# One start address for all streamed operands, and one for all kept ones, in the MLP and the output projection

## The chip, the cores and the metric

The kernel runs on one core of one Trainium2 chip. The metric is the device time of one execution in microseconds (us), as the median of several runs. A profile is one execution of its own; its span runs from the core's first instruction to its last. A core has TensorE (PE; its weight loads are listed apart as PEld), VectorE (DVE), ScalarE (ACT), GpSimd (POOL) and SyncE (SP), which issues the transfers. The engines run their own instructions in order and wait for each other by semaphores. On-chip memory has 128 partitions; an address here is a byte offset within a partition, the same in all 128. "Residue" means the address mod 256.

## The reference, cut to what matters

One decoder layer in float32 over 272 tokens (16 meta tokens and 256 real ones) of width 2048:

```
u    = rmsnorm(h) ;  proj = u @ w_in                # 2048 x 6144
o    = differential attention (8 heads) and stick-breaking attention (8 heads)
mixed = concat(rmsnorm(o_diff) * 0.8, rmsnorm(o_sb))
h    = h + mixed @ w_out                            # 2048 x 2048
m    = rmsnorm(h)
hid  = square(relu(m @ w_up))                       # 2048 x 8192
h    = h + hid @ w_down                             # 8192 x 2048
```

The output is h for the 256 real tokens.

## The kernel before

**Products in three parts.** Every large operand x is split into hi (x rounded to the matrix unit's float32r) and lo = x - hi. A product of two operands is three matmuls into the same accumulator, a *trio*: hi by hi, and hi by lo in both ways. A matmul has a *kept* operand (`lhsT`, 128 columns, loaded by a weight load ahead of it) and a *streamed* one (`rhs`, 256, 272 or 512 columns of 4 bytes).

**Weights in pieces.** All weights come in pieces of 128 x 1024 floats (512 KB). SyncE loads a piece into one of five `raw` buffers (L232); ScalarE rounds it into `whi` (L179), VectorE subtracts it into `wlo` (L181). The split pieces stand in rings of three buffers, in the MLP of five. A ring buffer has 1024 + 4 x 16 floats, so that a piece may begin 0, 64 or 128 bytes into it: `offset(g)` gives this for each piece.

**Stages.** (1) The input projection "in" streams `u` and keeps the weights (L983 to L985), with the attention heads worked in between. (2) The output projection "out", about 340 to 433 us: it keeps 128 tokens of `mixed` and streams 512 columns of `w_out` (`triple`, L1074). (3) The MLP in 8 rounds of 1024 hidden features. "up" keeps weights and streams 256 tokens of `m` (`triple2`, L1068). "down" keeps 128 tokens of the hidden activations and streams weights (`triple`, L1074), in 22 of 32 units by a fast scheme of 7 products of 256 columns in place of 8 (pieces "a" and "b", for which VectorE also makes sums of weights and activations), in the other units by plain products of 512 columns. Up pieces of round r+1 and down pieces of round r alternate in an order written out by hand (`order`, `mix`); which job each engine is given when comes from `Pace`, a small planner with a cost per operation. Neither looks at addresses.

**Writers of the kept operands.** In "out", a head's norm writes `mixed[:, k]`, 256 elements for hi and 256 for lo. In the MLP, `up_evac` writes the hidden activations of one group of features in eight slots of 128 tokens: ScalarE copies 8 x 128 elements into hi (L897), VectorE subtracts into lo (L899). Before, all hi parts of `mixed` and of `hid` stand first and all lo parts after them, 16 floats further than they would need to (`two_parts`). `m` has the layout of `u`: hi at 0 and lo 272 floats further.

**Accumulator copies.** In the fast down scheme ScalarE copies accumulators out and in again between units (L930, L935).

Of the kernel before, what the change touches and what calls it, by code (L numbers as in the profile page):

```python
# [7 lines left out]
F32 = mybir.dt.float32  # L8
F32R = mybir.dt.float32r
# [4 lines left out]
P = 128  # L14
DM = 2048
SEQ = 256
META = 16
TOK = META + SEQ
KT = DM // P
EPS = 1e-6  # L20
NEG = -1e30
ROW = 576
LINE = 16
ROUNDS = 8
PAIRS = 4
# [97 lines left out]
def hymba_layer(ctx: ExitStack, tc: tile.TileContext, xT_d, xh_d, win_d, wout_d, wup_d, wdn_d, cst_d, par_d, out_d):  # L123
    nc = tc.nc
    cp = ctx.enter_context(tc.tile_pool(name="const", bufs=1))
    big = ctx.enter_context(tc.tile_pool(name="big", bufs=1))
    wp = ctx.enter_context(tc.tile_pool(name="weights", bufs=1))
# [25 lines left out]
    def retile(tag, shape, name):  # L153
        return rtile(tag, shape, name, SLOTS["e"])

    def two_parts(x, k, n):

        return x[:, :, : k * n].rearrange("p a (k n) -> p k a n", n=n)


    par = cp.tile([P, G_END], F32, name="par")
    cst = tp.tile([P, C_ID], F32, bufs=1, name="cst")
# [1 line left out]
    xT = big.tile([P, KT, TOK], F32, tag="x", name="xT")  # L164
    big.tile([P, LINE], F32, name="pad_act")
    um = big.tile([P, KT, ROW], F32R, tag="act", name="u")[:, :, : 2 * TOK].rearrange("p k (a n) -> p k a n", a=2)
    big.tile([P, 2 * LINE], F32, name="pad_mix")
    mixed = two_parts(big.tile([P, 2, KT * SEQ + LINE], F32R, tag="mix", name="mixed"), KT, SEQ)

    def split_u(k):  # L170
        g = par[:, G_MIX + k : G_MIX + k + 1]
# [13 lines left out]
    strips = []  # L185
# [35 lines left out]
    def source(g):  # L221
        what, *at = order[g]
        if what == "in":
            (_, a, b), c = strips[at[0]], at[1]
            return win_d[a, b][:, 4 * c : 4 * c + 4]
        return {"out": wout_d, "up": wup_d, "a": wdn_d}[what][tuple(at)]

    raws, parts, raw_at, done_at, parted = {}, {}, {}, {}, set()
    dma = [1700.0]

    def load(dst, src, n):
        nc.sync.dma_start(dst, src)  # L232
        dma[0] = max(dma[0], pc.pe + 1700) + n * 1.42
        return dma[0] + 400

    def fetch(number, pieces=1):
        if number < len(loads):
            g = loads[number]
            if not raws:
                wp.tile([P, 3 * LINE], F32, name="pad_w")  # L240
            raws[g] = wp.tile([P, 4, 256], F32, tag="raw", bufs=RAW, name=f"raw_{g}")
            n = 4 // pieces
            for i in range(pieces):
                k = slice(n * i, n * i + n)
                raw_at[g, i] = load(raws[g][:, k], source(g)[:, k], n * 256)
                yield

    ring = {g: g - PARTS for g in range(len(order))}

    def offset(g):  # L250

        what, *at = order[g]
        if what == "in":
            return LINE if strips[at[0]][1] in (0, 3) else 0
        return LINE if what == "up" and at[1:] in ([0, 0], [2, 0]) else 0  # L260

    def part(g, pieces=1):
        if g < len(order) and g not in parts:
            pool, bufs, tag = wp, PARTS, "w"
            if g >= first_mlp:
                ring[g] = max(g - MLP_PARTS, first_mlp - PARTS + (g - first_mlp) % MLP_PARTS) if (g - first_mlp) % MLP_PARTS < PARTS else g - MLP_PARTS
                if (g - first_mlp) % MLP_PARTS >= PARTS:
                    pool, bufs, tag = mp, MLP_PARTS - PARTS, "v"
                    ring[g] = ring[g] if g - MLP_PARTS >= first_mlp else -1
            at = offset(g)  # L270
            hi, lo = (
                pool.tile([P, 1024 + 4 * LINE], F32R, tag=tag + x, bufs=bufs, name=f"w{x}_{g}")[:, n : n + 1024]
                .rearrange("p (k n) -> p k n", k=4)
                for x, n in (("hi", at), ("lo", at + LINE))
            )
            parts[g] = (hi, lo)
            what, *at = order[g]
            fast = what in "ab" and (at[0], at[1]) in FAST
            pc.job("weights", (fast_a if what == "a" else fast_b)(g, hi, lo) if fast else halves(g, hi, lo, pieces))
# [31 lines left out]
    def halves(g, hi, lo, pieces):  # L311
        n = 4 // pieces
        for i in range(pieces):
            src = (g, i) if (g, i) in raw_at else (g, 0)
            while src not in raw_at or ring[g] >= 0 and ring[g] not in done_at:
                yield pc.pe + 200, None
            yield max(raw_at[src], done_at.get(ring[g], 0.0)), "a"
            k = slice(n * i, n * i + n)
            t = yield from split(hi[:, k], lo[:, k], raws[g][:, k], 256 * n)
            for kk in range(n * i, n * i + n):  # L320
                pc.at["w", g, kk] = t
        parted.add(g)
# [3 lines left out]
    g = 0  # L326
    for c in range(4):
        n = 2 if c == 0 else 4
# [474 lines left out]
    m = H = mp = None  # L803
# [42 lines left out]
    def mlp_norm():  # L846

        yield from pc.until(*[("ss", u) for u in range(4)])
        yield pc.pe, "v"
        v = sp.tile([P, 2], F32, tag="n0", bufs=1, name="mlp_v")  # L850
        nc.vector.tensor_reduce(v, ss, axis=AX.X, op=ALU.add)
        nc.vector.tensor_scalar(v, v, 1.0 / DM, EPS, op0=ALU.mult, op1=ALU.add)
        nc.vector.reciprocal(R2, v)
        pc.at["R2"] = pc.V(2, 0.96, pc.V(8, 0.96, pc.V(8)))

    def mtile(tag, shape, name, bufs=1, dt=F32):
        return mp.tile(shape, dt, tag=tag, bufs=bufs, name=name)

    FULL = 8 if FAST else 4
    hid, Z = {}, {}  # L860

    def hidden(r):
        if r == 1:
            mp.tile([P, 3 * LINE], F32, name="pad_hid")
        if r % 2:
            x = mtile("hid", [P, 2, PAIRS * FULL * P + LINE], f"hid_{r}", 1, F32R)
        else:
            x = big.tile([P, 2, KT * SEQ + LINE], F32R, tag="mix", name=f"hid_{r}")
        hid[r] = two_parts(x, PAIRS * FULL, P).rearrange("p (q s) a n -> p q s a n", q=PAIRS)

    def up_evac(r, i, o):

# [91 lines left out]
    def banks(tag, n, name):  # L964
        while sum(t <= pc.pe for t in pc.banks[tag]) < n:
            pc.pe += 100
            pc.pump()
        pc.banks[tag] = sorted(pc.banks[tag])[n:]
        return [bank(tag, f"{name}_{j}") for j in range(n)]
# [52 lines left out]
    for g in range(LEAD + 1):  # L1022
        part(g, 2)
# [8 lines left out]
    def begin(g, lead):  # L1032

        if g:
            for later_g in range(g + 1, g + lead + 1):
                if later_g <= g + LEAD or later_g >= first_mlp:
                    part(later_g, 2 if later_g < 6 else 1)
        if g in load_of:
            pc.job("fetch", later(load_of[g] + LEAD + RAW))

    for s, c, kks in units:
        g = index["in", s, c]
        if c == 0 and kks[0] == 0:
            open_strips[s] = strip_start(s)
        out = open_strips[s]
# [3 lines left out]
        hi, lo = parts[g]  # L1049
        for j in range(2):  # L1050
            for kk in kks:
                k = 4 * c + kk
# [8 lines left out]
    def after(t, gen):  # L1061
        yield t, None
        yield from gen
# [6 lines left out]

    def triple(out, x, w, first, last, check=False):

        for i, (a, b) in enumerate(((1, 0), (0, 0), (0, 1))):
            nc.tensor.matmul(  # L1074
                out, lhsT=x[a], rhs=w[b], start=first and i == 0, stop=last and i == 2, skip_group_check=check
            )
        n = out.shape[-1]
        return pc.T(3 * (n / 2.4 + 2.5))

    for g in range(index["out", 0, 0], first_mlp):  # L1080
        _, u, c = order[g]
        if c == 0:
            out = banks("acc", 2, f"out_{u}")
            if u == 0:
                m = big.tile([P, KT, ROW], F32R, tag="act", name="m")[:, :, : 2 * TOK].rearrange("p k (a n) -> p k a n", a=2)[:, :, :, :SEQ]
        if u == 1 and c == 0:
            while pc.lanes["head"][0] or any(("mixed", k) not in pc.at for k in range(KT)):
                pc.pe += 100
                pc.pump()
            attention.close()  # L1090
            mp = ctx.enter_context(tc.tile_pool(name="mlp", bufs=1))
            mp.tile([P, MLP_PAD * LINE], F32, name="pad_mlp")
        begin(g, LEAD)
        hi, lo = (x.rearrange("p (k a) b -> p k (a b)", k=2) for x in parts[g])
        for kk in range(2):
            k = 2 * c + kk
            pc.stall(("w", g, 2 * kk + 1), ("mixed", k))
            for i in range(2):
                x = [mixed[:, k, a, P * i : P * i + P] for a in range(2)]
                t = triple(out[i], x, (hi[:, kk], lo[:, kk]), k == 0, k == KT - 1)  # L1100
                pc.pump()
        done_at[g] = pc.pe
        if c == 7:
            pc.job("evac", after(t, out_evac(u, out)))
            if u == 3:
                pc.job("once", mlp_norm())

    for g in range(first_mlp, len(order)):
        what, r, u, p = order[g]
        begin(g, MLP_LEAD)  # L1110
        hi, lo = parts[g]
        pc.stall(("w", g, 3))
        if what == "up":
# [3 lines left out]
            for j in range(2):  # L1117
                for kk in range(4):
                    k = 2 * p + kk % 2 + 8 * (kk // 2)
# [6 lines left out]
        else:  # L1126
            fast = (r, u) in FAST
            pc.stall(("hid", r, p))
            x = lambda slot: [hid[r][:, p, slot, a] for a in range(2)]
# [88 lines left out]
```

## Time and profile before

| | |
|---|---|
| median of 3 runs | 1131.67 us (1131.6 to 1132.87) |
| profiled execution, its own time | 1131.64 us |
| its span | 1129.9 us |
| TensorE busy | 1121.4 us, 8599 matmuls |
| weight loads busy | 1075.7 us, 8599 |
| VectorE busy | 947.2 us, 1459 instructions |
| ScalarE busy | 798.4 us, 1283 instructions |
| granted TensorE clock | 1.00 |
| read from HBM, written | 206.49 MB, 2.10 MB |

A matmul's listed duration is its passage from first column to last result, and passages overlap. How fast products follow each other is read from the chain of work that ended last, where runs of equal products stand with their length and count. "Idle before" in a group of instructions is time in which the engine had nothing to run, with the engine and line that ended it.

### The profile page before, as it was taken

To read this page: it belongs to the slowest core of one execution; us is meant where nothing else is said; L and a number is where in the kernel's file an instruction comes from. 1 tells how busy PE (TensorE), PEld (TensorE's weight loads), DVE (VectorE), ACT (ScalarE), POOL (GpSimd) and SP (SyncE) were. 2 spreads that over 40 slices of the span, in tenths; PEclk is the share of its full clock that TensorE was granted. 3 is DMA by queue.
4 is the path that set the end of the run, shared out by engine and by line. 5 is a ranking of instruction groups with operands and counts; after the bars stand their busy time and mean duration, and the time that the engine had idled before them with its cause. 6 is when DMAs were issued, how large, how long until landed. Compare 5 with 4: busy or idle time off the path is not lost.

```text
span 1129.9 us, 21823 instructions
## 1 busy us (share of the span) xinstructions
PE 1121.4 (99%) x8599; PEld 1075.7 (95%) x8599; DVE 947.2 (84%) x1459; ACT 798.4 (71%) x1283; POOL 1.1 (0%) x8
## 2 busy tenths in 40 slices
PE   8999999999999999999999999999999999999998
PEld 7999999999998889999999999999999999999987
DVE  6988988888876556698898899888889888888997
ACT  7779888788776445566577677677677677777663
POOL 0000000000000000000000000000000000000000
PEclk9999999999999999999999999999999999999999
DMA  8564544555545556555556555555555655655653
GB/s 332 185 225 133 156 143 150 150 162 154 156 148 171 182 187 212 180 179 194 196 187 207 190 186 199 200 189 190 203 187 195 215 187 187 222 183 193 209 179 135
DMA packets 58134, 210.00 MB, mean 186 GB/s; under 512 B 6576, under 2 KB 6832, under 8 KB 57904
## 3 DMA queue, kind: packets, MB, share of 16 engines
q1 hardware_dynamic: 58032, 208.61, 56.2%
q8 instruction: 67, 1.10, 0.4%
q14 instruction: 35, 0.29, 0.1%
HBM read 206.49 MB, written 2.10 MB: 185 GB/s over the span
## 4 chain that ended last, share of the span: by engine, by line
PE 97%; DMA 1%; ACT 1%; SPq 0%; DVE 0%; issue 0%; ACTq 0%
PE up L1068 32%; PE down L1074 28%; PE acc L983 8%; PE acc L985 8%; PE acc L984 8%; PE out L1074 8%; DMA xT<-in_x 1%; PE s_d L630 1%; PE po_s L670 1%; PE po_d L670 1%; PE z_s L630 1%; SPq L232 0%; PE pt L834 0%; PE pq_dq L558 0%; ACT whi L179 0%
## 5 line engine op out<-in xcount | busy, mean ns | idle before, releaser
L181 DVE TENSOR_TENSOR wlo<-raw,whi 128x1024 fp32r<-128x1024 f32 (+2 forms) x478 | 539.5, 1158 | 117.0 <-ACT whi L179 115.4
L179 ACT CAST whi<-raw 128x1024 fp32r<-128x1024 f32 (+2 forms) x478 | 466.2, 998 | 215.9 <-PE up L1068 63.2
L1068 PE MATMUL up<-m,whi 128*128 128x256 f32 x2048 | 366.6, 279 | 0.0
L1074 PE MATMUL down<-whi,hid 128*128 128x256 f32 (+1 forms) x1552 | 321.7, 304 | 0.7 <-ACT down L935 0.7
L1068 PEld LDWEIGHTS up<-m,whi 128*128 128x128 f32 x2048 | 314.9, 188 | 2.0
L1068 PE MATMUL up<-m,wlo 128*128 128x256 f32 x1024 | 287.0, 280 | 0.0
L1074 PEld LDWEIGHTS down<-whi,hid 128*128 128x128 f32 x1552 | 246.4, 188 | 13.5 <-ACT down L935 0.9
L1074 PE MATMUL down<-wlo,hid 128*128 128x256 f32 (+1 forms) x776 | 234.6, 302 | 0.0
L983 PE MATMUL acc<-u,whi 128*128 128x272 f32 (+1 forms) x768 | 222.4, 290 | 1.4 <-ACT whi L179 1.4
L985 PE MATMUL acc<-u,wlo 128*128 128x272 f32 (+1 forms) x768 | 219.0, 285 | 1.2 <-DVE wlo L181 1.2
L984 PE MATMUL acc<-u,whi 128*128 128x272 f32 (+1 forms) x768 | 217.4, 283 | 0.0
L1068 PEld LDWEIGHTS up<-m,wlo 128*128 128x128 f32 x1024 | 192.3, 188 | 0.0
L1074 PEld LDWEIGHTS down<-wlo,hid 128*128 128x128 f32 x776 | 145.5, 188 | 7.1
L983 PEld LDWEIGHTS acc<-u,whi 128*128 128x128 f32 x768 | 144.4, 188 | 3.0 <-ACT whi L179 2.1
L985 PEld LDWEIGHTS acc<-u,wlo 128*128 128x128 f32 x768 | 144.2, 188 | 1.8 <-DVE wlo L181 1.8
L984 PEld LDWEIGHTS acc<-u,whi 128*128 128x128 f32 x768 | 144.4, 188 | 0.0
L1074 PE MATMUL out<-whi,mixed 128*128 128x512 f32 x256 | 80.8, 397 | 0.0
L295 DVE TENSOR_TENSOR raw<-raw 128x512 f32<-128x512 f32 x88 | 60.9, 692 | 3.0
L1074 PEld LDWEIGHTS out<-whi,mixed 128*128 128x128 f32 x256 | 47.2, 188 | 10.1
L1074 PE MATMUL out<-wlo,mixed 128*128 128x512 f32 x128 | 50.5, 394 | 0.0
L879 ACT ACTIVATE hx<-up 128x512 f32<-128x512 f32 x32 | 19.1, 596 | 44.1 <-PE up L1068 44.1
L930 ACT COPY z<-down 128x512 f32<-128x512 f32 (+1 forms) x88 | 45.8, 528 | 3.0 <-PE down L1074 3.0
(241 smaller groups left out, 918.8 us busy)
## 6 DMA issues: line engine op xcount, KB each, us to landing
raw<-in_wup SPq DMA_DIRECT2D x128, 512.0 KB, 4.6
raw<-in_wdn SPq DMA_DIRECT2D x128, 512.0 KB, 3.7
raw<-in_win SPq DMA_DIRECT2D x95, 512.0 KB, 3.6
raw<-in_wout SPq DMA_DIRECT2D x32, 512.0 KB, 3.5
H<-in_xh SPq DMA_DIRECT2D x1, 2048.0 KB, 8.2
out<-H SPq DMA_DIRECT2D x8, 256.0 KB, 2.0
xT<-in_x SPq DMA_DIRECT2D x3, 544.0 KB, 9.8
cst<-in_cst SPq DMA_DIRECT2D x1, 609.0 KB, 11.0
```

Of the source, the lines that this page charges most:

```text
L179: nc.scalar.copy(hi, src)
L181: nc.vector.tensor_tensor(lo, src, as32(hi), op=ALU.subtract)
L295: nc.vector.tensor_tensor(raw[:, 3::-3], first, raw[:, 3:1:-1], op=ALU.add)
L630: nc.tensor.matmul(dst, lhsT=q[x][rows, cols], rhs=k[y][rows, :n], start=i == 0, stop=i == 2)
L670: nc.tensor.matmul(o, lhsT=l, rhs=r, start=i == 0, stop=i == len(todo) - 1)
L879: nc.scalar.activation(x[:, 0:4].rearrange("p a b -> p (a b)"), o, AF.Relu)
L930: nc.scalar.copy(Z[u][:, at], o[i][:, :n])
L983: nc.tensor.matmul(o, lhsT=h, rhs=xh, start=first, stop=False)
L984: nc.tensor.matmul(o, lhsT=h, rhs=xl, start=False, stop=False)
L985: nc.tensor.matmul(o, lhsT=l, rhs=xh, start=False, stop=last)
L1068: nc.tensor.matmul(out, lhsT=w[a], rhs=x[:, b], start=first and i == 0, stop=last and i == 2, skip_group_check=True)
L1074: nc.tensor.matmul(out, lhsT=x[a], rhs=w[b], start=first and i == 0, stop=last and i == 2, skip_group_check=check)
```

## The change

The layout of operands in memory changes, and the order of two matmuls in `triple`. In residues, as the built programs lay the tiles (three values: the three products of a trio in their order):

| products | streamed before | kept before | streamed now | kept now |
|---|---|---|---|---|
| up | 224, 32, 224 | 160, 160, 224 | 224, 224, 224 | 160, 160, 160 |
| up, pieces with (i, p) = (0, 0) and (2, 0) | 224, 32, 224 | 224, 224, 32 | 224, 224, 224 | 224, 224, 224 |
| down, fast and plain | 160, 160, 224 | 160, 96, 96 | 224, 224, 224 | 160, 160, 160 |
| out | 160, 160, 224 | 160, 96, 96 | 224, 224, 224 | 160, 160, 160 |
| in | unchanged | | | |

The first of the 32 pieces of "out" streams from 160 now. To get there:

- `mixed` and `hid` hold hi and lo of each block side by side ([..., 2, 256] and [..., 2, 128]) in place of all hi and then all lo. A write of `hid` by L897 or L899 now has 8 stretches of 128 elements with gaps of 128 between them, where it had one stretch of 1024; a write of `mixed` stays one stretch.
- `m` has hi and lo 256 floats apart in place of 272.
- `offsets(g)` gives hi and lo of a piece the same offset in the MLP and in "out": 0 where the piece is kept (up, but for the pieces named), 64 bytes where it is streamed.
- `triple` begins with hi by hi and then lo by hi, where it began with lo by hi.
- Padding tiles of 64 to 192 bytes are added or fall away, so that the tiles begin where the table needs them.

No instruction is added or removed on any engine, and apart from that swap inside `triple` each engine's instructions stand in the order of before. The transfers are the same.

```diff
-    def two_parts(x, k, n):
-        return x[:, :, : k * n].rearrange("p a (k n) -> p k a n", n=n)
...
-    big.tile([P, 2 * LINE], F32, name="pad_mix")
-    mixed = two_parts(big.tile([P, 2, KT * SEQ + LINE], F32R, tag="mix", name="mixed"), KT, SEQ)
+    big.tile([P, 3 * LINE], F32, name="pad_mix")
+    mixed = big.tile([P, KT, 2, SEQ], F32R, tag="mix", name="mixed")
...
-            if not raws:
-                wp.tile([P, 3 * LINE], F32, name="pad_w")
...
-    def offset(g):
+    def offsets(g):
...
         what, *at = order[g]
         if what == "in":
-            return LINE if strips[at[0]][1] in (0, 3) else 0
-        return LINE if what == "up" and at[1:] in ([0, 0], [2, 0]) else 0
+            line = strips[at[0]][1] in (0, 3)
+            return line * LINE, line * LINE + LINE
+        line = at[1:] in ([0, 0], [2, 0]) if what == "up" else at != [0, 0] if what == "out" else True
+        return line * LINE, line * LINE
...
-            at = offset(g)
...
-                for x, n in (("hi", at), ("lo", at + LINE))
+                for x, n in zip(("hi", "lo"), offsets(g))
...
     def hidden(r):
-        if r == 1:
-            mp.tile([P, 3 * LINE], F32, name="pad_hid")
         if r % 2:
-            x = mtile("hid", [P, 2, PAIRS * FULL * P + LINE], f"hid_{r}", 1, F32R)
+            hid[r] = mtile("hid", [P, PAIRS, FULL, 2, P], f"hid_{r}", 1, F32R)
         else:
-            x = big.tile([P, 2, KT * SEQ + LINE], F32R, tag="mix", name=f"hid_{r}")
-        hid[r] = two_parts(x, PAIRS * FULL, P).rearrange("p (q s) a n -> p q s a n", q=PAIRS)
+            hid[r] = big.tile([P, PAIRS, FULL, 2, P], F32R, tag="mix", name=f"hid_{r}")
...
     def triple(out, x, w, first, last, check=False):
-        for i, (a, b) in enumerate(((1, 0), (0, 0), (0, 1))):
+        for i, (a, b) in enumerate(((0, 0), (1, 0), (0, 1))):
...
-                m = big.tile([P, KT, ROW], F32R, tag="act", name="m")[:, :, : 2 * TOK].rearrange("p k (a n) -> p k a n", a=2)[:, :, :, :SEQ]
+                m = big.tile([P, KT, ROW], F32R, tag="act", name="m")[:, :, : 2 * SEQ].rearrange("p k (a n) -> p k a n", a=2)
```

## The prediction

> **What bounds the kernel now.** I began with the page's busy shares and its costliest groups, went on to the chain that ended last, and ended with the chain in two windows and the stretches of the run.
>
> ```profile
> PE 1121.4 (99%) x8599; PEld 1075.7 (95%) x8599; DVE 947.2 (84%) x1459; ACT 798.4 (71%) x1283; POOL 1.1 (0%) x8
> PE 97%; DMA 1%; ACT 1%; SPq 0%; DVE 0%; issue 0%; ACTq 0%
> ```
>
> TensorE carries 97% of the chain. The span is 1129.9 us and the profiled execution took 1131.64 us, so 1.7 us lie around the span; the median of the runs, 1131.67 us, is the same time. What TensorE waits for is small:
>
> ```profile
> PE acc L983 <- ACT whi L179: 1.4, 2, 0.9
> PE warm L1013 <- DVE idle L1010: 1.2, 1, 1.2
> PE acc L985 <- DVE wlo L181: 1.2, 3, 0.7
> PE down L1074 <- ACT down L935: 0.7, 1, 0.7
> ```
>
> These are all its waits, 4.5 us in total, and only the last 0.7 us lie in the part that the change touches. No edit can gain by removing a wait. The time is the number of products times the distance between two product starts, and the change can only move that distance. The products that it touches, shape by shape:
>
> ```profile
> L1068 PE MATMUL up<-m,whi 128*128 128x256 f32 x2048 | 366.6, 279 | 0.0
> L1068 PE MATMUL up<-m,wlo 128*128 128x256 f32 x1024 | 287.0, 280 | 0.0
> L1074 PE MATMUL down<-whi,hid 128*128 128x256 f32 x1232 | 221.9, 280 | 0.7 <-ACT down L935 0.7
> L1074 PE MATMUL down<-wlo,hid 128*128 128x256 f32 x616 | 171.2, 278 | 0.0
> L1074 PE MATMUL down<-whi,hid 128*128 128x512 f32 x320 | 100.1, 394 | 0.0
> L1074 PE MATMUL out<-whi,mixed 128*128 128x512 f32 x256 | 80.8, 397 | 0.0
> L1074 PE MATMUL down<-wlo,hid 128*128 128x512 f32 x160 | 63.4, 397 | 0.0
> L1074 PE MATMUL out<-wlo,mixed 128*128 128x512 f32 x128 | 50.5, 394 | 0.0
> ```
>
> That makes 2048 + 1024 + 1232 + 616 = 4920 products of 256 columns, and 320 + 160 + 256 + 128 = 864 of 512. The mean of one (279 ns) is its whole passage and overlaps the next; the distance comes from runs in the chain of waits, whose columns are start, length, and what stood there how often:
>
> ```profile
> 350.88 17.50 PE out L1074 x75
> 372.73 18.70 PE out L1074 x81
> 432.76 7.07 PE up L1068 x60
> 443.18 38.50 PE up L1068 x327
> 481.68 2.80 PE down L1074 x12
> 487.31 2.47 PE down L1074 x21
> ```
>
> 256 columns: 38.50 us / 327 = 117.7 ns in the up products, 2.47 / 21 = 117.6 ns in the fast down products. 512 columns: 2.80 / 12 = 233.3 ns in the plain down products, 17.50 / 75 = 233.3 ns in one stretch of the output projection and 18.70 / 81 = 230.9 ns in another. Together the touched products take about 4920 x 117.7 = 579 us and 864 x 232.5 = 201 us: 780 us of the span. One nanosecond on each 256-wide product is 4.9 us, or 0.43% of the time.
>
> **The change part by part.**
>
> *The addresses.* Before, the streamed operands of one trio start at residues 224, 32, 224 (up) or 160, 160, 224 (down, out) mod 256, so a start lies 0, +64 or -64 bytes from the one ahead; while a product streams, the kept operand of the next one lies 64 bytes below it. Afterwards every start is 224 and every kept operand 160. The distance of 64 bytes between a streamed operand and the next kept one is thus the same before and after (but in the up pieces 0,0 and 2,0, where it is 0 in both kernels). New is only that consecutive streams and consecutive kept operands begin alike. I look for what the trace says of such starts. The up trio (steps +64, -64, 0) and the fast down trio (0, +64, -64, other residues) have 117.7 and 117.6 ns. The run of 60 up products at 432.76 us begins with piece 0,0, whose distance is 0 and not 64: 7.07 / 60 = 117.8 ns. Three patterns of addresses thus lie within 0.2 ns, which is 1 us over 4920 products. From this I take 0 for the 256-wide products. Both ends stay open, since no long run of before has one start for all streams. The nearest rows where it has are the attention's output products, whose streamed operand stays at residue 128 and kept one at 0:
>
> ```profile
> L670 PE MATMUL po_s<-ah_s,vh_s 128*128 128x256 f32 x8 | 2.3, 283 | 0.0
> L670 PE MATMUL po_d<-ah_d,vh_d 128*128 128x256 f32 x8 | 2.3, 282 | 0.0
> L670 PE MATMUL po_s<-al_s,vh_s 128*128 128x256 f32 x8 | 2.2, 281 | 0.0
> L670 PE MATMUL po_d<-al_d,vh_d 128*128 128x256 f32 x8 | 2.2, 280 | 0.0
> L670 PE MATMUL po_d<-ah_d,vl_d 128*128 128x256 f32 x8 | 2.2, 280 | 0.0
> L670 PE MATMUL po_s<-ah_s,vl_s 128*128 128x256 f32 x8 | 2.2, 279 | 0.0
> ```
>
> Their mean is 280.8 ns against 279.3 ns for the four 256-wide rows above: 1.5 ns more, and 1.5 x 4920 = 7.4 us if the distance follows the passage. They are only 48 products, in runs of a few that start after other work, and their kept operand lies 128 bytes off, so I leave this as the upper end. The lower end comes from the output projection: its two stretches at 350.88 and 372.73 us have the same addresses mod 256 and yet differ by 2.4 ns of 233.3, or 1.0%. The stream thus has a tighter and a looser rhythm, and where it enters decides. If one start for all brought the tight rhythm everywhere, it would be 1.0% of 117.7 = 1.2 ns on 4920 products (5.9 us), 2.4 ns on the 480 plain down products (1.2 us), and 2.4 ns on the third or so of the 384 output products that run loosely now (0.3 us): 7.4 us.
>
> *The order within a trio* of the down and output products: before, kept lo, hi, hi against streamed hi, hi, lo; now kept hi, lo, hi. It is the same three products into the same accumulator. A load of the kept operand stands ahead of every product before (8599 of each in the first row) and none goes away, so it costs 0; it only sets which addresses follow each other, which is priced above. Every other instruction of every engine keeps its place.
>
> *The hidden activations and the mixed heads, hi and lo side by side.* For the mixed heads each write stays one stretch of 256 elements. For the hidden activations the ScalarE copy (L897) and the VectorE subtraction (L899) now write 8 stretches of 128 with gaps, and L899 reads its second operand so:
>
> ```profile
> L899 DVE TENSOR_TENSOR hid<-hx,hid 128x1024 fp32r<-128x1024 f32 x32 | 39.0, 1219 | 0.2 <-ACT hid L897 0.2
> L299 DVE TENSOR_TENSOR raw<-raw 128x256 f32<-128x256 f32 x88 | 37.4, 425 | 3.0
> L887 DVE TENSOR_TENSOR hx<-hx 128x256 f32<-128x256 f32 x32 | 13.5, 422 | 7.4 <-ACT hx L883 7.1
> L889 DVE TENSOR_TENSOR hx<-hx 128x128 f32<-128x128 f32 x32 | 9.4, 292 | 1.1
> L897 ACT CAST hid<-hx 128x1024 fp32r<-128x1024 f32 x32 | 33.4, 1045 | 2.0 <-DVE hx L891 2.0
> ```
>
> L887 writes two stretches of 128 with a gap and takes 422 ns, L299 one stretch of 256 and 425 ns: gaps cost nothing there, and I take 0. The upper end is eight separate instructions of 128, 8 x 292 = 2336 ns, or 1.1 us more on each of 32. The lower end is 0, as no row shows a gap that gains more than those 3 ns. What hides it is room on the engines in the mixed stage:
>
> ```profile
> 482.00:1080.00 598.00, 598.00 (x4751) 582.82 (x4750) 530.39 (x690) 421.74 (x541) 0.00 (x0) 1.00 0.59 195
> ```
>
> The columns are the stretch, then busy time of PE, weight loads, VectorE and ScalarE, and the granted clock, 1.00. TensorE is busy in all 598 us, VectorE in 530 and ScalarE in 422. Even 32 x 1.1 = 36 us more would leave VectorE 32 us of room over the stage. Without that cover the accumulator copies (L935) would be late next, the only thing TensorE waits for there, and at worst 36 us would show.
>
> *The split of the weights* (ScalarE L179, VectorE L181) keeps its shapes, and its destinations move by 0 or 64 bytes:
>
> ```profile
> L181 DVE TENSOR_TENSOR wlo<-raw,whi x478: 683/1218/1229, 5.6 to 1115.2; 128x1024 fp32r<-128x1024 f32 x126, 128x768 fp32r<-128x768 f32 x30, 128x512 fp32r<-128x512 f32 x4
> L179 ACT CAST whi<-raw x478: 603/1047/1072, 5.0 to 1113.3; 128x1024 fp32r<-128x1024 f32 x126, 128x768 fp32r<-128x768 f32 x30, 128x512 fp32r<-128x512 f32 x4
> ```
>
> These are minimum, median and maximum in ns. Both offsets occur among the 478, and the longest stands within 11 ns (L181) and 25 ns (L179) of the median: 0, and hidden like the above; 25 ns on each of some 350 pieces of the touched parts would be 9 us of ScalarE's 176 us of room.
>
> The Trainium skill speaks against any effect: "TensorE: Matmul & The Clock Gate", section "Step-by-step: what each phase is for", gives TensorE two independent read ports, one for the streamed operand and one for the weights, so that loading the next weights takes nothing from the running product. By that rule addresses cost nothing and the sum stays at 1131.6 us. The trace does not quite bear the page out, since two stretches with equal shapes run at 233.3 and 230.9 ns; none of its rows can tell whether the ports are the reason.
>
> The sum: 1131.64 + 0 + 0 + 0 + 0 = 1131.6 us, with ends of -7.4 and +7.4 us from the addresses.
>
> **The rivals.**
>
> *Tight rhythm.* With one start for all streams each product repeats the one before and the stream falls into the rhythm of 230.9 ns per 512. For it: that rhythm exists, at the same shapes and addresses. Against it: in the up and down products, with the same 64 bytes to the next kept operand, no stretch of before shows a 1% faster one. 1131.6 - 7.4 = 1124.2 us.
>
> *One start is the worse one.* The steps of 64 bytes between streams keep a stream's head off the place that the one ahead read last; with equal starts head and tail meet, in every product of the MLP and the output projection. For it: the attention rows with 1.5 ns more. Against it: a third of the steps of before is already 0, so that two products of three at most could still lose, and in the distance of 117.7 ns nothing shows that the third loses. 1131.6 + 7.4 = 1139.0 us, slower; it decides against the forecast from 0.46 ns per 256-wide product on (0.2%, or 2.3 us, over 4920).
>
> *The writers become the bound.* The gapped writes take eight times an instruction of 128, and the stage's VectorE work bunches so that TensorE waits for a piece. For it: VectorE is at 89% in the mixed stage. Against it: L887. Were half of the 36 us to show, 1131.6 + 18 = 1150 us.
>
> **How the numbers follow.** No change: 0.45. Tight rhythm, in whole or in a part over 0.2%: 0.31. One start is worse: 0.22. The writers: 0.02. About 0.2% (2.3 us) is what a measurement of this kernel can tell from no change, so faster 0.31, same 0.45, slower 0.24. The likeliest time is 1131.6 us. Its own range is 1129.4 to 1133.9 us. The range for 8 in 10 takes in the full price of the tight rhythm and nearly that of the worse start: 1124 to 1138 us. What is left out is half of the worst case on the slow side, the writers, and a gain larger than any rhythm in the trace.
>
> **What would show it.** In the chain of waits after: up pieces of 24 products in 2.83 us, 21 down products in 2.47 us, 12 plain ones in 2.80 us say no change; 2.80, 2.44 and 2.77 us say tight rhythm; 2.86 us and more for 24 say that one start is worse. The mean of L899 should stay at 1219 ns and of L897 at 1045 ns; at 2300 ns the writers' rival has its price. New waits of TensorE in the MLP would show that it is not a matter of distances at all. I am wrong if the distance of the 256-wide products moves by more than half a nanosecond, either way.

## The result, and the profile after

The changed kernel takes 1110.97 us (1110.76 to 1112.3) against 1131.63 us for the kernel before on the same chip: a ratio of 0.982, 95% interval 0.980 to 0.984. It is 20.7 us faster. The profiled execution has a span of 1109.2 us, where before had 1129.9.

The first lines of the page after, busy time and share of the span, show the same numbers of instructions, and less TensorE time:

```profile
PE 1100.9 (99%) x8599; PEld 1057.5 (95%) x8599; DVE 945.1 (85%) x1459; ACT 795.9 (72%) x1283; POOL 1.1 (0%) x8
```

TensorE's busy time falls from 1121.4 to 1100.9 us, by 20.5. VectorE and ScalarE lose 2 us or so. The chain of waits after, in the window of the output projection and the first MLP round (start, length, what, count):

```profile
350.98 17.18 PE out L1066 x75
...
372.49 18.56 PE out L1066 x81
...
431.95 6.94 PE up L1060 x60
...
442.25 37.87 PE up L1060 x327
480.11 2.75 PE down L1066 x12
482.86 2.72 PE up L1060 x24
485.58 2.38 PE down L1066 x21
```

24 up products take 2.72 us, or 113.3 ns each, where they took 2.83 us (117.9). 21 fast down products take 2.38 us (113.3) in place of 2.47 us (117.6), 12 plain ones 2.75 us (229.2) in place of 2.80 (233.3). In the output projection both long stretches now stand at 229.1 ns (17.18 / 75 and 18.56 / 81), where one stood at 233.3 and one at 230.9. How much that is in all stands in the shares of the chain by line, first before (1129.9 us):

```profile
by line: PE up L1068 32.0%; PE down L1074 28.5%; PE acc L983 8.2%; PE acc L985 8.1%; PE acc L984 7.9%; PE out L1074 7.9%; DMA xT<-in_x 0.9%; PE s_d L630 0.6%; PE po_s L670 0.6%; PE po_d L670 0.5%; PE z_s L630 0.5%; SPq L232 0.4%; PE pt L834
```

and after (1109.2 us):

```profile
by line: PE up L1060 31.7%; PE down L1066 28.1%; PE acc L975 8.6%; PE acc L977 8.5%; PE acc L976 8.3%; PE out L1066 8.0%; PE s_d L625 0.6%; DMA raw<-in_win 0.6%; PE po_s L665 0.6%; PE po_d L665 0.5%; PE z_s L625 0.5%; DVE wlo L177 0.4%; PE 
```

The up products go from 32.0% of 1129.9 us to 31.7% of 1109.2 us, or 361.6 to 351.6 us; the down products of both kinds from 28.5% to 28.1%, or 322.0 to 311.7 us. The shares are rounded to 0.1%, about 1 us; within that, these two, 20.3 us, are nearly the whole gain of 20.7. TensorE's waits stayed: they are

```profile
PE acc L975 <- ACT whi L175: 1.2, 2, 0.8
PE warm L1005 <- DVE idle L1002: 1.2, 1, 1.2
PE down L1066 <- ACT down L927: 1.2, 1, 1.2
PE acc L977 <- DVE wlo L177: 0.7, 3, 0.2
```

4.3 us in total, as before (4.5). The writers with gaps cost nothing: 1219 ns before and after on VectorE, 1045 and 1048 on ScalarE:

```profile
L891 DVE TENSOR_TENSOR hid<-hx,hid 128x1024 fp32r<-128x1024 f32 x32 | 39.0, 1219 | 0.3 <-ACT hid L889 0.2
L889 ACT CAST hid<-hx 128x1024 fp32r<-128x1024 f32 x32 | 33.5, 1048 | 2.7 <-DVE hx L883 2.7
```

One row did not fit the plain reading "alike addresses are faster". The run of 327 up products takes 37.87 us, which is 115.8 ns each and not 113.3. Three windows within that run, from its first part, its middle and its end, give its length and count there:

```profile
442.96 12.13 PE up L1060 x103
...
455.80 2.51 PE up L1060 x21
...
458.99 19.09 PE up L1060 x168
```

Its first part, behind two pauses in which TensorE transposes for `m`, still runs at 117.8 ns (12.13 / 103), at the very residues that give 113.6 ns later (19.09 / 168). In between, at 119.5 ns, stands piece (0,2,0), one of the sixteen up pieces whose kept operand begins at the streamed one's residue (distance 0; every other product of the MLP has 64). The experiments went after that.

### The profile page after: what moved, and what is told of

It reads as the page before. It is cut to its first block, busy times and chain, and to the rows that moved or that the text cites. A ratio compares the mean times of both kernels' runs of the same rounds, so it can differ in the third digit from the quotient of the medians.

```text
span 1109.2 us, 21822 instructions
## 1 busy us (share of the span) xinstructions
PE 1100.9 (99%) x8599; PEld 1057.5 (95%) x8599; DVE 945.1 (85%) x1459; ACT 795.9 (72%) x1283; POOL 1.1 (0%) x8
## 4 chain that ended last, share of the span: by engine, by line
PE 98%; DVE 1%; DMA 1%; ACT 0%; SPq 0%; issue 0%; DVEq 0%
PE up L1060 32%; PE down L1066 28%; PE acc L975 9%; PE acc L977 8%; PE acc L976 8%; PE out L1066 8%; PE s_d L625 1%; DMA raw<-in_win 1%; PE po_s L665 1%; PE po_d L665 1%; PE z_s L625 1%; DVE wlo L177 0%; PE pt L829 0%; PE pq_dq L553 0%; SPq L228 0%; DVE H L899 0%
## 5 line engine op out<-in xcount | busy, mean ns | idle before, releaser
L1060 PE MATMUL up<-m,whi 128*128 128x256 f32 x2048 | 356.7, 277 | 0.0
L1066 PE MATMUL down<-whi,hid 128*128 128x256 f32 (+1 forms) x1552 | 313.1, 300 | 1.2 <-ACT down L927 1.2
L1060 PEld LDWEIGHTS up<-m,whi 128*128 128x128 f32 x2048 | 311.4, 188 | 1.9
L1060 PE MATMUL up<-m,wlo 128*128 128x256 f32 x1024 | 284.0, 277 | 0.0
L1066 PE MATMUL down<-wlo,hid 128*128 128x256 f32 (+1 forms) x776 | 233.3, 301 | 0.0
```

Source lines behind the costliest of these rows:

```text
L1060: nc.tensor.matmul(out, lhsT=w[a], rhs=x[:, b], start=first and i == 0, stop=last and i == 2, skip_group_check=True)
L1066: nc.tensor.matmul(out, lhsT=x[a], rhs=w[b], start=first and i == 0, stop=last and i == 2, skip_group_check=check)
```

## The experiments

Each kernel ran beside the kernel before on the same chip (1130.9 to 1131.8 us); a time without a range is that of one execution. "Fast rhythm" means 113.3 ns between 256-wide products, "slow rhythm" a mean of 117.8 ns. A "zero piece" is an up piece of distance 0.

**Streams alike alone, and kept operands alike alone.** The change makes both alike. `streams` starts from the kernel before:

```diff
-                m = ...[:, :, : 2 * TOK].rearrange("p k (a n) -> p k a n", a=2)[:, :, :, :SEQ]
+                m = ...[:, :, : 2 * SEQ].rearrange("p k (a n) -> p k a n", a=2)
-                for x, n in (("hi", at), ("lo", at + LINE))
+                for x, n in (("hi", at), ("lo", at + (LINE if order[g][0] in ("in", "up") else 0)))
```

> The kernel before, with the streamed operands alike within up and within down and out (up 224, 224, 224 against kept 160, 160, 224; down and out 160, 160, 160 against kept 160, 96, 96, in the order of before). The kept operands still have two residues, so that the distance from a stream down to the next kept operand is 64, 0, 64 within a trio. If equal starts of the streams are what gained: 256-wide products about 113.3 ns apart as after the change, and about 1111 us. If equal kept operands gained: 117.7 ns as before and 1131.6 us. If each product has its own price by its distance to the kept operands (113.3 ns at 64, 120 ns at 0, as the pieces (0,0) and (2,0) show after the change): a mean of 115.6 ns and about 1121 us.

`kept` starts from the kernel after; `m` goes back to its old layout and

```diff
-        return line * LINE, line * LINE
+        return line * LINE, line * LINE + (0 if what == "up" else LINE)
...
-        for i, (a, b) in enumerate(((0, 0), (1, 0), (0, 1))):
+        for i, (a, b) in enumerate(((1, 0), (0, 0), (0, 1))):
```

> The kernel after the change, with the streams as uneven as before (up 224, 32, 224; down and out 224, 224, 32, lo by hi first) and all kept operands at 160. If equal starts of the streams gained: about 117.7 ns and 1131.6 us. If equal kept operands gained: 113.3 ns and 1111 us. If both are needed, or each product has its own price: between them, at 1118 to 1131.6 us.

`streams` took 1131.7 us, `kept` 1130.2 us, the kernel before beside them 1131.5. The chain of waits of `streams`:

```profile
485.23 2.83 PE up L1068 x24
488.06 2.48 PE down L1074 x21
```

and of `kept`:

```profile
484.44 2.82 PE up L1060 x24
487.27 2.48 PE down L1066 x21
```

Neither half brings anything on the 256-wide products: both stand at 2.82 to 2.83 us for 24. So neither half is enough alone. Each half, though, also puts a third of the products at another distance to the next kept operand (0 in `streams`, 128 bytes in `kept`), so these two kernels can't tell uneven starts from uneven distances; the kernel before, with uneven starts and 64 bytes in all but the zero pieces, is slow as well. A price per product by its own distance (about 1121 us for `streams`) falls too.

**The trio's order.** `old_order` is the kernel after with the old order in `triple`, lo by hi first.

> The kernel after the change with the order of a trio in down and output products as before (lo by hi first). All residues stay alike, so all theories expect no change from the kernel after: 1111 us. Only if the order itself gained would it go back towards 1131 us.

1110.1 us: the order gains nothing.

**Without zero pieces.**

```diff
-        line = at[1:] in ([0, 0], [2, 0]) if what == "up" else at != [0, 0] if what == "out" else True
+        line = False if what == "up" else at != [0, 0] if what == "out" else True
```

> The kernel after the change, with the up pieces (0,0) and (2,0) kept at 160 like all others, so that every product of the MLP has the distance of 64 bytes. Theory A, the price hangs on the addresses alone: the 384 products of these pieces go from 120 to 113.3 ns, 2.6 us less, 1108.4 us. Theory B, the rhythm has a memory (in the profile after the change the up pieces just behind a pause, 450 to 466 us, run at 117.8 ns with the same addresses, and run at 113.3 ns only behind the next piece of distance 0): without the pieces of distance 0 the slow rhythm stays from the pause on, about 4400 products by 4.45 ns less the 0.8 us of the pieces themselves, so about 1130 us.

1127.7 us: 17 us of the gain are gone, though now every product of the MLP has the same residues as the fast ones of the kernel after. Its chain of waits:

```profile
431.26 7.07 PE up L1060 x60
...
441.68 38.51 PE up L1060 x327
480.19 2.75 PE down L1066 x12
482.94 2.83 PE up L1060 x24
485.77 2.47 PE down L1066 x21
```

2.83 and 2.47 us, the slow rhythm of the kernel before, while the 512-wide products keep 2.75 us for 12. The time lies 2 us from the 1130 of theory B and 19 us from the 1108.4 of theory A. So theory A, that the price hangs on the addresses alone, falls: equal residues allow two rhythms, and which one runs is carried on from what ran ahead.

One place at the end of this run the theories did not have. Behind its last pause (a wait of 0.7 us for ScalarE's accumulator copy, L927, that ends at 1085.5 us), short runs of 256-wide down products alternate with 512-wide ones:

```profile
1088.69 0.39 PE L1066 MATMUL down<-whi,hid 128*128 128x256 f32 x2
...
1089.93 0.28 PE L1066 MATMUL down<-wlo,hid 128*128 128x256 f32 x1
1090.05 0.39 PE L1066 MATMUL down<-whi,hid 128*128 128x512 f32 x1
```

The 12 products of 256 columns from 1088.69 to 1090.05 us follow each other by 113.3 ns, and so do the later ones: the fast rhythm, with no zero piece in the MLP. In the kernel after, the products behind the same pause run at 118 ns to the end, though they were at 113.3 ahead of it. A pause can thus be followed by either rhythm, and a zero piece is not the only way into the fast one.

**One zero piece, early and late.** `one_zero` has a single one, the first whole piece behind the last of the two pauses:

```diff
-        line = at[1:] in ([0, 0], [2, 0]) if what == "up" else at != [0, 0] if what == "out" else True
+        line = at == [0, 1, 1] if what == "up" else at != [0, 0] if what == "out" else True
```

> The kernel after the change with one single up piece at distance 0 in place of sixteen: piece (0,1,1), the first whole one behind the last pause at the start of the MLP. If one piece sets the fast rhythm and it lasts until the next pause: 15 pieces of 24 products less at 120 ns (15 x 24 x 6.67 ns = 2.4 us) and three pieces of 24 earlier in the fast rhythm (0.3 us), so 1108.3 us, 2.0% faster than before. If the fast rhythm wears off and every round must set it anew: towards 1127.7 us, which the kernel with no such piece took.

`late_zero` has it at `[4, 0, 0]`.

> The kernel after the change with one single up piece at distance 0, not at the start of the MLP but as the first up piece of round 4. By the theory that one such piece sets the fast rhythm for all that follows: 2172 products of 256 columns between the place of the single piece in the kernel that took 1108.0 us and this one stay at 117.8 in place of 113.3 ns, so 1108.0 + 2172 x 4.46 ns = 1117.7 us, and the up runs of the chain of waits change from 2.83 to 2.72 us for 24 products just behind the piece. If the fast rhythm of that kernel came from elsewhere (its start, a pause): 1108 or 1127.7 us, and no step at the piece.

`one_zero` took 1107.99 us (1107.92 to 1109.28), a ratio to before of 0.980, interval 0.978 to 0.981: the expected 1108.3 within its spread, and no execution of it was as slow as the fastest of the kernel after (1110.76). The fast rhythm, once set, lasts to the end: all 97 runs of 24 up products in its chain stand at 2.72 us, where in `no_zero` all 97 stand at 2.83. `late_zero` took 1117.5 us against 1117.7 expected, and its chain of waits shows the switch:

```profile
719.20 2.83 PE up L1060 x24
...
732.90 2.47 PE down L1066 x21
735.37 2.87 PE up L1060 x24
738.24 2.75 PE down L1066 x12
740.99 2.72 PE up L1060 x24
743.71 2.38 PE down L1066 x21
```

The row of 2.87 us is the zero piece itself, at 120 ns. Ahead of it all 24s take 2.83 us, behind it 2.72. That a zero piece sets the fast rhythm at a distance of 64 bytes is therefore shown, at three places in the program: (0,2,0), (0,1,1) and (4,0,0).

**Other distances.** Four kernels put the streams 32, 96, 128 and 192 bytes from the kept operands, with the sixteen zero pieces. For 128:

```diff
-        line = at[1:] in ([0, 0], [2, 0]) if what == "up" else at != [0, 0] if what == "out" else True
+        line = 2 * (at[1:] in ([0, 0], [2, 0]) if what == "up" else at != [0, 0] if what == "out" else True)
...
-                m = ...[:, :, : 2 * SEQ].rearrange("p k (a n) -> p k a n", a=2)
+                m = ...[:, :, 1 * LINE : 1 * LINE + 2 * SEQ].rearrange("p k (a n) -> p k a n", a=2)
```

The others have 3 x 16 floats (192), 24 (96) and 8 (32) in place of the 2 x 16, and `m` begins 32, 8 and 56 floats in.

> The kernel after the change, with every stream of the MLP and the output projection 128 bytes from the kept operands in place of 64 (pieces (0,0) and (2,0) still at distance 0). If equal starts are all that counts: 1111 us, the same. If the distance of 64 bytes counts too: another rhythm; the attention's output products, which stand at 128 bytes and about 118 ns, let expect 1131 us.

> The kernel after the change with the streams 192 bytes from the kept operands (which is the kept operands 64 bytes above, mod 256), pieces (0,0) and (2,0) at distance 0. If what counts is that the weight load reads a place that the stream has already left (64 below), a place that the stream is about to reach is worse: 120 ns or more per 256-wide product, at least 1140 us. If only equal starts count and a zero-distance piece ahead: 1111 us. The kernel at 128 bytes took 1138 us.

> The kernel after the change with the streams 32 bytes from the kept operands in place of 64 (pieces (0,0) and (2,0) still at distance 0). If addresses matter in steps of 64 bytes, 32 bytes are the same step as 0 for half of each access: up to 120 ns per 256-wide product, about 1141 us. If 64 bytes are only one distance of many that do: 1111 us.

> The kernel after the change with the streams 96 bytes from the kept operands in place of 64 (pieces (0,0) and (2,0) still at distance 0). The kernel at 64 bytes runs at 113.3 ns per 256-wide product (1111 us), the one at 128 bytes near 118.8 ns (1138 us). If it goes by steps of 64 bytes, 96 lies with 64: 1111 us. If there is a slope: between them, about 1124 us. A distance with less than 113.3 ns would show here as less than 1111 us.

| distance | time, us | 24 up products, us | 12 plain down products, us |
|---|---|---|---|
| 32 | 1128.9 | 2.80 to 2.83 | 2.80 |
| 64 (the change) | 1111.0 | 2.72 | 2.75 |
| 96 | 1143.0 | 2.88 | 2.80 |
| 128 | 1138.1 | 2.85 to 2.88 | 2.78 to 2.80 |
| 192 | 1117.7 | 2.72 and 2.83 | 2.80 |

(The two columns on the right are from the chains of waits, 480 to 530 us, and for 192 from the rows below.) With the sixteen zero pieces 64 is the best of the five, and 96 and 128 are worse than the uneven addresses of before. 96 bytes do not go with 64, so it is not by steps of 64; 32 bytes are not as bad as 0 either. None of the times expected for 32, 96 and 128 bytes came, and 192, expected to be the worst, was the second best. The 120.0 ns at 96 and the 119.2 at 128 are means: single distances there run from 112 to 126 ns. All four kernels move the streams and leave the other kept operands at 160, so a rule by distance is not told apart from one by the streams' own residue; the zero pieces, whose kept operands move with the streams, stand at 119.5 to 120.0 ns at all five residues. The chain of waits at 192 bytes shows both rhythms within one round:

```profile
771.11 2.38 PE down L1066 x21
773.49 2.88 PE up L1060 x24
776.37 2.47 PE down L1066 x21
778.84 2.83 PE up L1060 x24
...
784.14 2.83 PE up L1060 x24
786.97 2.80 PE down L1066 x12
789.77 2.73 PE up L1060 x24
```

At 192 bytes the zero piece (2.88) ends the fast rhythm, and the plain down products (2.80 for 12) set it again. That is the reverse of 64 bytes, and it could be tested.

**192 bytes without zero pieces.** The kernel at 192, with `False if what == "up"` in place of the condition.

> The kernel with the streams 192 bytes from the kept operands (1117.7 us), now without the up pieces at distance 0. In its profile the chain shows a distance-0 piece (2.88 us for 24) followed by 2.83 us for 24 products, and a plain down piece of 512 columns (2.80 us for 12) followed by 2.72 us: there the plain pieces set the fast rhythm and the distance-0 pieces end it. If so, without them all 256-wide products behind the first plain down piece run at 113.3 ns: about 800 slow products by 4.46 ns (3.5 us) and 384 by 6.7 ns (2.6 us) less, 1111.6 us. If pieces of distance 0 are always what sets the fast rhythm: no fast rhythm, and about 1132 us.

1110.6 us, 7 us less. Its chain of waits:

```profile
433.11 6.82 PE up L1060 x60
...
440.36 2.48 PE up L1060 x21
...
443.28 37.08 PE up L1060 x327
480.36 2.79 PE down L1066 x12
483.15 2.73 PE up L1060 x24
```

The first run of up products stands at 113.7 ns: behind the 512-wide output products the fast rhythm is there already, earlier than the expectation had it, which may be the microsecond by which it is under 1111.6. But the 21 products between the two pauses are slow (2.48 us, with single distances of 117 to 120 ns behind the first), and the 327 behind the second pause fast again (113.4), with no 512-wide product and no zero piece in between. In `far192`, at the same residues, it is the other way about: the 21 take 2.40 us and the products behind the second pause run at 117.8 ns. At 192 bytes, too, a pause can be followed by either rhythm. What removes 17 us of the gain at 64 bytes gains 7 us at 192.

**The input projection alike too.**

```diff
-            return line * LINE, line * LINE + LINE
+            return line * LINE, line * LINE
...
-ROW = 576
+ROW = 640
...
-    um = big.tile([P, KT, ROW], F32R, tag="act", name="u")[:, :, : 2 * TOK].rearrange("p k (a n) -> p k a n", a=2)
+    um = big.tile([P, KT, ROW], F32R, tag="act", name="u").rearrange("p k (a n) -> p k a n", a=2)
```

> The kernel after the change with the input projection laid out alike too: the lo part of its streamed operand 320 floats behind the hi part (a row of 640 floats in place of 576), and both parts of a weight piece at one residue 64 bytes below. No piece of distance 0 stands in that stage, and attention work pauses the stream every few products. By the theory that the rhythm has a memory and a pause brings the slow one: 256-wide input products stay at 117.8 ns and the 272-wide ones near 123.3 ns, 1111 us. If equal addresses alone suffice there: 4.4 ns less on 768 products and 3.3 ns less on 1536, 8.5 us, so 1102.5 us.

1113.58 us (1113.03 to 1114.03), a ratio to before of 0.984, interval 0.983 to 0.986: 2.6 us more than the kernel after, so alike addresses in this stage rather cost something. The groups of TensorE's instructions by shape, the input projection after the change:

```profile
L975 PE MATMUL acc<-u,whi 128*128 128x272 f32 x512 | 149.9, 293 | 0.0
L977 PE MATMUL acc<-u,wlo 128*128 128x272 f32 x512 | 147.1, 287 | 0.0
L976 PE MATMUL acc<-u,whi 128*128 128x272 f32 x512 | 146.3, 286 | 0.0
L975 PE MATMUL acc<-u,whi 128*128 128x256 f32 x256 | 72.6, 284 | 1.2 <-ACT whi L175 1.2
```

and in `in_alike`:

```profile
L975 PE MATMUL acc<-u,whi 128*128 128x272 f32 x512 | 151.4, 296 | 0.0
L977 PE MATMUL acc<-u,wlo 128*128 128x272 f32 x512 | 147.9, 289 | 0.0
L976 PE MATMUL acc<-u,whi 128*128 128x272 f32 x512 | 147.9, 289 | 0.0
L975 PE MATMUL acc<-u,whi 128*128 128x256 f32 x256 | 72.3, 283 | 1.2 <-ACT whi L175 1.2
```

The passage of the 272-wide products gets 2 to 3 ns longer, that of the 256-wide ones stays; the mean distance of the 272-wide ones within their runs goes from 126.2 to 128.9 ns. Neither of the two times expected (1111 and 1102.5 us) came. A stream of 272 columns is 1088 bytes, which is not a multiple of 256, so it ends 64 bytes further round than it began; that this is why alike starts do not help there is argued, not shown.

**What is shown and what is open.** Shown: the distance between products depends on the residues of streamed and kept operands together, and for equal residues on what ran ahead; there are at least two rhythms at 64 and at 192 bytes. The three distances 113.3, 117.8 and 120.0 ns lie at 0, 4.5 and 6.7 ns from the shortest, that is 0, two thirds and one of 6.7 ns. It is tempting to read this as an extra halt of fixed length in none, two of three and all products, when a weight load and the stream ahead want the same place in memory. The starts of the single products, which the traces have to the nanosecond, speak against it: in `no_zero` all 2560 distances inside the up runs behind 480 us lie at 117 to 119 ns, and none near 113 or 120; in `one_zero` all lie at 113 or 114. So in `no_zero` each product comes about 4.5 ns later than in `one_zero`, not two of three. In `kept` the same mean comes from distances near 115, 118 and 120 ns. What the delay is stays open. Why 64 and 192 bytes allow the fast rhythm and 96 and 128 do not stays open, and so does what decides the rhythm behind a pause: at 64 bytes the two pauses at the start of the MLP were followed by the slow one in every kernel, the last pause by either. In the kernel after, the first piece of the output projection has distance 0 too; whether the 229.1 ns of that stage need it, no run tells.

## Why the prediction was wrong

*What bounds the kernel.* Right: the products' distance, with nothing to gain from waits. TensorE's waits stayed at 4.3 us, and the 20.7 us came from the distance alone.

*The addresses.* Here it failed, at "From this I take 0 for the 256-wide products". The step took three patterns of addresses within 0.2 ns as a sign that addresses do not matter. What the runs showed in its place: the three agreed because all ran in the slow rhythm, whose mean uneven addresses (`streams`, `kept`) and even ones without a zero piece (`no_zero`) share at 2.82 to 2.83 us per 24. Equal numbers from three patterns of one family say nothing on a pattern outside it, and "New is only that consecutive streams and consecutive kept operands begin alike" named just that. The distance moved by 4.5 ns, not 0.

*The two ends.* The lower end, 7.4 us, was the term that was mis-sized. As a bound it was too small by 13 us. It rested on the right observation, two rhythms at equal addresses in the output projection, and on the thought that the rhythm depends on where the stream enters. But it carried that 1.0% of a 512-wide product over to the 256-wide ones as a percentage, 1.2 ns; they measured 4.5 ns, nearly four times as much. Carried over as time per product, 2.4 ns, it would have given 12 us and still been short. The plain down products, priced at 2.4 ns, measured 4.1 (2.80 to 2.75 us for 12). The upper end, from the attention's rows, was no guide to 64 bytes. Those rows stand at 128, and the kernel at 128 bytes took 1138.1 us where the end was 1139.0, but that is luck as far as is known: read as a distance, the same rows gave about 118 ns, and 1131 us was expected of that kernel.

*The zero pieces.* The prediction saw that pieces (0,0) and (2,0) have distance 0 in both kernels and used them only as a third pattern. They were the part on which 17 of the 20.7 us hang. Nor is their 117.8 ns a price of distance 0 as such: in the kernel before, with uneven starts, the zero pieces among the runs of 24 stand at 118.1 ns, and in the kernel after at 120.0.

*The rivals.* The tight rhythm was the right one in direction, at 1124.2 us in place of 1111, and in half of its mechanism: there is a tighter rhythm that products keep up. That equal starts alone make the stream fall into it is wrong, for without zero pieces they leave it slow (1127.7 us). Its "against", that no stretch of before showed a faster one in the up and down products, was true and weak: before had no such addresses. That one start is the worse one fell at 64 bytes; at 96 and 128 its direction holds, and no run tested its reason, a head and a tail that meet.

*The writers, the split, the order of the trio.* Right at 0: 1219 ns before and after for the gapped VectorE writes, 1045 and 1048 on ScalarE, and 1110.1 us with the old order.

*The rule of the Trainium skill* ("TensorE: Matmul & The Clock Gate", "Step-by-step: what each phase is for"), by which weight loads take nothing from the running stream, gave 1131.6 us. The runs differ from it: with shapes, order and counts the same, addresses alone moved the time between 1108.0 and 1143.0 us, and the measurement decides. That it is the two reads that meet is argued, not shown.

## What to carry to other kernels

Where TensorE runs back to back, lay out all streamed operands at one start mod 256 and all kept ones 64 bytes lower, hi and lo parts included, and then read the distance between products off the chain of waits in every stage, since the same addresses ran at 113.3 and at 117.8 ns. If a stage is in the slow rhythm, try one short stretch with kept and streamed operand at the same residue behind the pause ahead of it (1127.7 against 1108.0 us here), and test it per distance, because at 192 bytes it did the opposite. All this was measured with 256-column float32r products, each behind a weight load. When a price is bounded from rows, ask whether the rows are of one family; three equal numbers from patterns that share a property are one observation.

## What was not expected of the hardware

The distance between equal products carries a memory: `no_zero` and `one_zero` differ by one piece of 24 products out of 8599 and by 19.7 us. The rhythm that this piece set held for over 600 us, through thousands of products of two widths. And a pause can switch it either way, at the same residues. Moving the same streams by 32 bytes, from 64 to 96, cost 32 us (1111.0 to 1143.0).
